# The MLPs' tiles of high and low weight parts begin 0 to 112 bytes further on

## The chip, the cores and the metric

The kernel runs on one core of a Trainium2 chip. The metric is the device time of one execution in microseconds (us), the median of several runs. The engines that matter here are TensorE (PE in the profile; its weight loads are PEld), VectorE (DVE), ScalarE (ACT) and the DMA queue of SyncE (SPq).

## What is computed

A two-layer transformer on 256 tokens of width 2,048 in float32: a layer with stick-breaking attention, a layer with native sparse attention, and behind each an MLP with a squared ReLU:

```python
def sqrelu_mlp(h, w1, w2):
    return jnp.square(jax.nn.relu(h @ w1)) @ w2        # w1: 2048 x 8192, w2: 8192 x 2048

for layer in range(2):
    h = h + attention[layer](rms_norm(h, ...))
    h = h + sqrelu_mlp(rms_norm(h, mlp_norm_g[layer]), mlp_w1[layer], mlp_w2[layer])
```

All weights are float32, some 400 MB, and each is read from memory once.

## The kernel before

**Split products.** TensorE multiplies numbers of type fp32r. To keep float32 accuracy each operand is split into a high part (the number rounded to fp32r) and a low part (what the rounding left). A product is then three: high by high, low by high, high by low. Activations are split once and stay in the tiles `xs` (high and low parts of the normed input side by side, 16 blocks of 128 rows, each 2 x 256 columns) and `yhi`, `ylo` (the MLP's hidden part). Weights come in chunks of 512 KB: `load` (L132) fetches one into one of five `raw` buffers, 128 partitions x 1,024 numbers, and `split` (L123 to L128) makes its parts: ScalarE copies `raw` into `hi` (L125), VectorE subtracts `hi` from `raw` into `lo` (L127). There are four buffers of each, taken in turn.

**The MLP.** Each MLP runs four rounds of `group1` and `group2`. `group1` makes 2,048 hidden columns in four blocks of 512, each from 8 chunks of `w1` in `proj_T2`: there the weights are the stationary operand, 8 matmuls of `hi` against 512 columns of `xs` (L193) and then 8 of `lo` against its 256 high columns (L199). `group2` multiplies with `w2`: 24 chunks go through `chunk_N`, where the activations are stationary and the weights move, 12 matmuls of 512 columns each (L147: `hi` against `yhi` and `ylo` in turn, then `lo` against `yhi`). Between these stand 8 chunks of one column block done with a Strassen scheme in `chunk_S`: 21 matmuls of 256 columns (L268). Three of its seven products use parts of the raw chunk, in the tiles `shi` and `slo`, which it splits by itself; the four others use sums of its quarters, `ts`, which go through `split` and so lie in `hi` and `lo` tiles. The stationary operand there is `ss` (sums of the activations) or `yhi`, `ylo`. Of the 12 matmuls with `hi` and `lo` tiles, 9 meet `ss` and 3 meet `yhi` or `ylo`. The list `order` in `group2` says in which order plain and Strassen chunks follow one another.

**Other users of `split`.** The attention layers' projections call it too: `chunk_T` (L176), `chunk_N` (L147) and `proj_T2h` (L213, L219).

**Where the tiles lie.** A tile is a stretch of bytes in each partition. In the built program, before and after, with the address modulo 128:

```
tile                      before                               after
xs                        32,896 (0)                           the same
yhi, ylo                  65,664 and 82,048 (0)                the same
raw, 5 buffers            108,480 + 4,096 b (64)               the same
hi, 4 buffers             128,960 + 4,096 b (64)               128,960 + 4,224 b (64) + offset
lo, 4 buffers             145,344 + 4,096 b (64)               145,856 + 4,224 b (64) + offset
ss                        161,728 (64)                         162,752 (64)
shi, slo                  218,048 and 221,120 (64)             219,072 and 222,144 (64)
```

Within a chunk all slices that a matmul takes begin a multiple of 512 bytes further on, so the address modulo 128 is that of the tile. In the attention layers some operands meet at other distances modulo 128: 0 on L642, L643 and L645; 0, 32, 64 and 96 in turn on L780 (`ws` moving, `bs` stationary); 32 on L919 and L920 where `vc` is an operand.

Of the kernel before, what the change touches and what calls it, by code (L numbers as in the profile page):

```python
# [9 lines left out]
F32R = mybir.dt.float32r  # L10
# [5 lines left out]
P = 128  # L16
# [3 lines left out]
KD = D // P  # L20
NB = 512
# [4 lines left out]
KC = 2  # L26
# [13 lines left out]
def hybrid_kernel(  # L40
# [10 lines left out]
    whi = ctx.enter_context(tc.tile_pool(name="whi", bufs=4))  # L51
    wlo = ctx.enter_context(tc.tile_pool(name="wlo", bufs=4))
# [52 lines left out]
    def pump():  # L105
        if beside:
            b = beside[0]
            b[2] += b[1] / KC
            while b[2] >= 1:
                b[2] -= 1  # L110
                y = next(b[0], b)
                if y is b:
                    beside.remove(b)
                if y:
                    break
# [4 lines left out]
                pass  # L120


    def split(raw):  # L123
        hi = whi.tile(raw.shape, F32R, tag="hi", name="hi")
        nc.scalar.activation(hi, raw, AF.Copy)  # L125
        lo = wlo.tile(raw.shape, F32R, tag="lo", name="lo")
        nc.vector.tensor_tensor(lo, raw, hi.bitcast(F32), op=OP.subtract)  # L127
        return hi, lo  # L128

# [7 lines left out]
    def load_split(*where):  # L137
        return split(load(*where))

    def bank(pool, tag):  # L140
        return pool.tile([P, NB], F32, tag=tag, name=tag)
# [44 lines left out]
    def proj_T2(ps, src, n0):  # L186


        for k0 in range(0, KD, KC):
            hi, lo = load_split(src, k0, KC, n0, NB)  # L190
            tiles = [(kk, m) for kk in range(KC) for m in range(NB // P)]
            for kk, m in tiles:
                nc.tensor.matmul(  # L193
                    ps[m], hi[:, kk, m * P:(m + 1) * P], xs[:, k0 + kk, :, :].rearrange("p a t -> p (a t)"),
                    start=k0 + kk == 0, stop=k0 + kk == KD - 1, skip_group_check=True,
                )
            pump()
            for kk, m in tiles:
                nc.tensor.matmul(  # L199
                    ps[m][:, :T], lo[:, kk, m * P:(m + 1) * P], xhi[:, k0 + kk, :],  # L200
                    start=False, stop=k0 + kk == KD - 1, skip_group_check=True,
                )
            pump()
# [75 lines left out]
    def banks_S(pool, tag):  # L279

        W = NB // 2
        bs = [bank(pool, tag) for _ in range(4)]
        half = lambda j, i: bs[j][:, i * W:(i + 1) * W]
        return bs, [half(0, 0), half(1, 0), half(1, 1), half(2, 0), half(2, 1), half(3, 1), half(3, 0)]
# [29 lines left out]
    def split_evac(hi, lo, src, scale=None):  # L314

        if scale is None:
            nc.scalar.activation(hi, src, AF.Copy)  # L317
            nc.vector.tensor_tensor(lo, src, hi.bitcast(F32), op=OP.subtract)  # L318
        else:
            nc.scalar.activation(hi, src, AF.Copy, scale=scale)  # L320
            nc.vector.scalar_tensor_tensor(
                lo, src, scale, hi.bitcast(F32), op0=OP.mult, op1=OP.subtract
            )
# [44 lines left out]
    def make_rstd(layer):  # L368
        s = small.tile([P, NT], F32, tag="ms", name="ms")
        nc.vector.tensor_reduce(s, ssq_t[layer], axis=AX.X, op=OP.add)  # L370
        nc.vector.tensor_scalar(s, s, 1.0 / D, EPS, op0=OP.mult, op1=OP.add)
        r = small.tile([P, NT], F32, tag="rstd", name="rstd")
        nc.gpsimd.tensor_tensor(r, s, neghalf[:, :NT], op=OP.pow)
        return r

    def bcast_rows(rstd):

        ps = bank(att, "att")
        for t in range(NT):
            nc.tensor.transpose(ps[:, t * P:(t + 1) * P], rstd[:, t:t + 1].to_broadcast([P, P]), ident)  # L380
        return ps
# [36 lines left out]
    def mlp(l, layer, junk, done, last=None):  # L418
        w1, w2 = mlp_w1[l], mlp_w2[l]
        ss = junk.tile([P, 2, KD // 2, 4, P], F32R, name="ss", bufs=1)  # L420
        row = junk.tile([P, T], F32, name="row", bufs=1)

        def rows():
            yield
            pb = bcast_rows(make_rstd(layer))
            nc.scalar.activation(row, pb[:, :T], AF.Copy)

        def group1(fg, pools):

            for fb in range(D // NB):  # L430
                ps = [bank(*pools[fb % 2]) for _ in range(NB // P)]
                proj_T2(ps, w1, fg * D + fb * NB)
                k, n = fb * (NB // P), NB // P
                a = junk.tile([P, n, T], F32, tag="pre", name="pre", bufs=1)
                for j in range(n):
                    c = junk.tile([P, T], F32, tag="part", name="part")
                    nc.scalar.activation(c, ps[j][:, T:], AF.Copy)
                    nc.vector.tensor_tensor(a[:, j, :], ps[j][:, :T], c, op=OP.add)
                nc.vector.scalar_tensor_tensor(
                    a, a, 0.0, row.unsqueeze(1).to_broadcast([P, n, T]), op0=OP.max, op1=OP.mult  # L440
                )
                s = junk.tile([P, n, T], F32, tag="sq", name="sq", bufs=1)
                nc.scalar.activation(s, a, AF.Square)
                nc.scalar.activation(yhi[:, k:k + n, :], s, AF.Copy)
                nc.vector.tensor_tensor(ylo[:, k:k + n, :], s, yhi[:, k:k + n, :].bitcast(F32), op=OP.subtract)

                sv = s.rearrange("p (j kk) t -> p j kk t", kk=2)
                a1, a2 = [[sv[:, :, kk, t * P:(t + 1) * P] for kk in (1, 0)] for t in range(NT)]
                q = junk.tile([P, 2, 4, P], F32, tag="sums", name="sums", bufs=1)
                nc.vector.scalar_tensor_tensor(q[:, :, 0, :], a2[0], -1.0, a2[1], op0=OP.mult, op1=OP.subtract)  # L450
                nc.vector.tensor_tensor(q[:, :, 2, :], a1[0], a2[0], op=OP.subtract)
                nc.vector.tensor_tensor(q[:, :, 1, :], a2[1], q[:, :, 2, :], op=OP.subtract)
                nc.vector.tensor_tensor(q[:, :, 3, :], a1[1], q[:, :, 1, :], op=OP.subtract)
                split_evac(ss[:, 0, k // 2:k // 2 + 2], ss[:, 1, k // 2:k // 2 + 2], q)

        def group2(fg, plain, strassen, end):

            NK = KD // KC
            order, si = [], 0
            for i in range(3 * NK):  # L460
                order.append(((0, 1, 3)[i // NK], i % NK))
                if si < NK and i >= (3 + 1.75 * si if end else 4 + 2.25 * si):
                    order.append((2, si))
                    si += 1
            for nb, i in order:
                k0 = fg * KD + i * KC
                args = (w2, k0, nb * NB, i == 0, i == NK - 1, yhi, ylo)
                if nb == 2:
                    if i == 0:
                        bs, s = banks_S(*strassen)  # L470
                    chunk_S(s, *args, ss[:, 0], ss[:, 1], koff=fg * KD)
                    if i == NK - 1:
                        add_S(nb, bs, s, junk)
                        if end:
                            for n in range(3):
                                done(n, strassen)
                    continue
                if i == 0:
                    ps = [bank(*plain) for _ in range(NT)]
                out = last is not None and end and nb == 3  # L480
                chunk_N(ps, w2, k0, nb * NB, i == 0, i == NK - (2 if out else 1), yhi, ylo, koff=fg * KD,
                        by_token=out and i == NK - 1)
                if i == NK - 1:
                    if out:
                        add_out(nb, ps, last)
                        return
                    add_h(nb, ps)
                    if end and nb == 3:
                        done(nb, plain)

        spawn(rows(), 1)
        A, B = (acc, "acc"), (att, "att")
        for fg in range(DFF // D):
            end = fg == DFF // D - 1
            group1(fg, ((A, B), (B, A))[fg % 2])
            group2(fg, *((A, B), (B, A))[fg % 2], end)
# [211 lines left out]
    with tc.tile_pool(name="nsa", bufs=2) as ap, ExitStack() as last:  # L708
# [270 lines left out]
        for k0 in range(0, KD, GK):  # L979
            raw = load(w_in, k0, GK, D + 6 * NB + GATES - P, P)  # L980
# [6 lines left out]
            for kk in range(GK):  # L987
                k = k0 + kk
# [40 lines left out]
        for g in range(G):  # L1029
            ps = [bank(acc, "acc") for _ in range(NT)]  # L1030
            for k0 in range(0, KD, KC):
                raw = wraw.tile([P, KC, NB], F32, tag="raw", name="raw")
# [61 lines left out]
```

## Time and profile before

| | us |
|---|---|
| median of 3 runs | 2201.02 (2199.73 to 2203.11) |
| the profiled execution | 2201.79 |
| its span, first to last instruction | 2200.1 |

The profile is of one execution. Its page gives each engine's busy time, the chain of work that ended last (followed back from the last instruction), and groups of instructions by line. Matmuls are pipelined: the record of one lasts past the start of the next, so the distance between two starts is shorter than a record.

### The profile page before, as it was taken

To read this page: it belongs to the slowest core of one execution; us is meant where nothing else is said; L and a number is where in the kernel's file an instruction comes from. 1 tells how busy PE (TensorE), PEld (TensorE's weight loads), DVE (VectorE), ACT (ScalarE), POOL (GpSimd) and SP (SyncE) were. 2 spreads that over 40 slices of the span, in tenths; PEclk is the share of its full clock that TensorE was granted. 3 is DMA by queue.
4 is the path that set the end of the run, shared out by engine and by line. 5 is a ranking of instruction groups with operands and counts; after the bars stand their busy time and mean duration, and the time that the engine had idled before them with its cause. 6 is when DMAs were issued, how large, how long until landed. Compare 5 with 4: busy or idle time off the path is not lost.

```text
span 2200.1 us, 31289 instructions
## 1 busy us (share of the span) xinstructions
PE 2187.0 (99%) x11922; PEld 1875.4 (85%) x11922; DVE 1537.9 (70%) x2096; ACT 1204.4 (55%) x1697; POOL 42.6 (2%) x75
## 2 busy tenths in 40 slices
PE   9999999999999999999999999999999999999998
PEld 9888888888888888888887888888888888888887
DVE  5656655677667677668777777756776776777775
ACT  5565665555455455455555666655554554554553
POOL 0000000000000000000000011000000000000000
PEclk9999999999999999999999999999999999999999
DMA  7655555665665665665667554456556656656654
GB/s 233 207 165 172 165 171 182 182 192 184 205 190 175 215 190 178 215 191 174 213 184 219 153 144 139 134 169 183 181 183 214 188 184 207 189 174 220 189 174 155
DMA packets 260767, 405.98 MB, mean 185 GB/s; under 512 B 13188, under 2 KB 91912, under 8 KB 260616
## 3 DMA queue, kind: packets, MB, share of 16 engines
q1 hardware_dynamic: 259800, 403.52, 60.2%
q8 instruction: 93, 1.52, 0.3%
q10 hardware_dynamic: 816, 0.46, 0.1%
q14 instruction: 58, 0.48, 0.1%
HBM read 401.83 MB, written 2.10 MB: 184 GB/s over the span
## 4 chain that ended last, share of the span: by engine, by line
PE 98%; DVE 1%; DMA 0%; POOL 0%; ACT 0%; issue 0%; DVEq 0%; ACTq 0%; POOLq 0%
PE acc L147 31%; PE att L147 13%; PE acc L193 11%; PE att L193 11%; PE acc L213 5%; PE acc L199 5%; PE att L199 5%; PE att L268 4%; PE acc L268 3%; PE acc L219 3%; PE acc L176 2%; PE att L926 1%; PE att L331 1%; PE att L918 0%; DMA raw<-in_mlp_w_dram 0%; PE att L919 0%
## 5 line engine op out<-in xcount | busy, mean ns | idle before, releaser
L127 DVE TENSOR_TENSOR lo<-raw,hi 128x1024 fp32r<-128x1024 f32 x687 | 836.6, 1222 | 380.3 <-ACT hi L125 358.1
L125 ACT ACTIVATE hi<-raw 128x1024 fp32r<-128x1024 f32 x687 | 724.8, 1057 | 656.3 <-PE acc L147 208.5
L193 PE MATMUL acc<-xs,hi 128*128 128x512 f32 x1024 | 259.8, 396 | 0.0
L193 PE MATMUL att<-xs,hi 128*128 128x512 f32 x1024 | 259.1, 395 | 0.0
L147 PE MATMUL acc<-hi,yhi 128*128 128x512 f32 x640 | 251.7, 394 | 0.0
L147 PE MATMUL acc<-hi,ylo 128*128 128x512 f32 x640 | 250.6, 392 | 0.0
L193 PEld LDWEIGHTS acc<-xs,hi 128*128 128x128 f32 x1024 | 183.0, 188 | 34.7 <-DVE h L387 0.3
L193 PEld LDWEIGHTS att<-xs,hi 128*128 128x128 f32 x1024 | 183.2, 188 | 34.5
L147 PE MATMUL acc<-hi,xs 128*128 128x512 f32 x704 | 178.6, 394 | 0.0
L147 PE MATMUL acc<-lo,yhi 128*128 128x512 f32 x640 | 174.1, 393 | 0.0
L147 PEld LDWEIGHTS acc<-hi,xs 128*128 128x128 f32 x704 | 130.5, 188 | 27.6
L147 PE MATMUL att<-hi,ylo 128*128 128x512 f32 x380 | 149.7, 394 | 0.0
L147 PE MATMUL att<-hi,yhi 128*128 128x512 f32 x380 | 149.4, 393 | 0.0
L199 PEld LDWEIGHTS acc<-xs,lo 128*128 128x128 f32 x1024 | 135.9, 188 | 11.6
L199 PEld LDWEIGHTS att<-xs,lo 128*128 128x128 f32 x1024 | 135.9, 188 | 11.6
L147 PEld LDWEIGHTS acc<-lo,yhi 128*128 128x128 f32 x640 | 119.6, 188 | 25.8 <-issue 0.4
L147 PEld LDWEIGHTS acc<-hi,ylo 128*128 128x128 f32 x640 | 120.3, 188 | 24.5 <-DVE ylo L318 0.2
L147 PEld LDWEIGHTS acc<-hi,yhi 128*128 128x128 f32 x640 | 120.2, 188 | 24.3 <-ACT yhi L317 0.2
L199 PE MATMUL acc<-xs,lo 128*128 128x256 f32 x1024 | 137.6, 277 | 0.0
L199 PE MATMUL att<-xs,lo 128*128 128x256 f32 x1024 | 137.5, 277 | 0.0
L243 DVE TENSOR_TENSOR ts<-raw 128x512 f32<-128x512 f32 x64 | 44.3, 692 | 128.9 <-DMA raw<-in_mlp_w_dram 128.9
L125 ACT ACTIVATE hi<-ts 128x1024 fp32r<-128x1024 f32 x64 | 67.9, 1061 | 114.4 <-DVE ts L248 86.3
(305 smaller groups left out, 3064.9 us busy)
## 6 DMA issues: line engine op xcount, KB each, us to landing
raw<-in_mlp_w_dram SPq DMA_DIRECT2D x512, 512.0 KB, 4.2
raw<-in_sb_w_qkv_dram SPq DMA_DIRECT2D x95, 512.0 KB, 4.2
raw<-in_nsa_w_in_dram SPq DMA_DIRECT2D x50, 512.0 KB, 3.6
raw<-in_sb_w_out_dram SPq DMA_DIRECT2D x32, 512.0 KB, 3.9
raw<-in_nsa_w_in_dram SPq DMA_DIRECT2D x64, 256.0 KB, 3.4
raw<-in_nsa_w_out_dram SPq DMA_DIRECT2D x32, 512.0 KB, 3.9
w1t<-in_nsa_cmp_w_dram SPq DMA_DIRECT2D x8, 512.0 KB, 4.8
h<-in_x_dram SPq DMA_DIRECT2D x8, 256.0 KB, 4.5
```

Source lines behind the costliest of these rows:

```text
L125: nc.scalar.activation(hi, raw, AF.Copy)
L127: nc.vector.tensor_tensor(lo, raw, hi.bitcast(F32), op=OP.subtract)
L147: mm = lambda a, b, k, t, s, e: nc.tensor.matmul(ps[t], a[:, k, t * P:(t + 1) * P], b, start=s, stop=e)
L176: nc.tensor.matmul(o, w[:, kk, m * P:(m + 1) * P], x[:, k0 + kk, :], start=s, stop=e, skip_group_check=True)
L193: nc.tensor.matmul(ps[m], hi[:, kk, m * P:(m + 1) * P], xs[:, k0 + kk, :, :].rearrange("p a t -> p (a t)"), start=k0 + kk == 0, stop=k0 + ...
L199: nc.tensor.matmul(ps[m][:, :T], lo[:, kk, m * P:(m + 1) * P], xhi[:, k0 + kk, :], start=False, stop=k0 + kk == KD - 1, skip_group_check=True,
L213: nc.tensor.matmul(ps[m], hi[:, kk, m * P:(m + 1) * P], xs[:, k0 + kk, :, :].rearrange("p a t -> p (a t)"), start=k0 + kk == 0, stop=k0 + ...
L219: nc.tensor.matmul(ps[m][:, :T], lo[:, kk, m * P:(m + 1) * P], xhi[:, k0 + kk, :], start=False, stop=k0 + kk == KD - 1, skip_group_check=True,
L243: nc.vector.tensor_tensor(ts[:, :2, :], flat[:, W:3 * W].rearrange("p (a n) -> p a n", a=2), b12, op=OP.subtract)
L268: nc.tensor.matmul(ps[i], a, w, start=s, stop=e, skip_group_check=True)
L331: nc.tensor.transpose(ps[:, j * T + t * P:j * T + (t + 1) * P], h[:, t, (kp + j) * P:(kp + j + 1) * P], ident)
L926: nc.tensor.transpose(ptp[:w, j * P:(j + 1) * P], src(j), ident)
```

## The change

`split` takes tiles of 1,024 + 32 numbers and uses 1,024 of them from an offset on. The offset comes from a list, `shift`, and is 0 where the list is empty. The MLP fills the list: in `group1` with 16 bytes x ((column block + chunk) modulo 8) for each chunk, in `group2` with 16 bytes x (place in the order modulo 8). High and low part of one chunk have the same offset. The order of the instructions on each engine is the same as before, and so are their waits. In the MLPs the address of `hi` and `lo` modulo 128 thus goes through all eight multiples of 16; on L193 and L199 each comes for one eighth of the matmuls.

```diff
+    shift = []
+
     def split(raw):
-        hi = whi.tile(raw.shape, F32R, tag="hi", name="hi")
+
+        n = KC * NB
+        o = shift.pop(0) if shift else 0
+        view = lambda t: t[:, o:o + n].rearrange("p (k n) -> p k n", k=raw.shape[1])
+        hi = view(whi.tile([P, n + 32], F32R, tag="hi", name="hi"))
         nc.scalar.activation(hi, raw, AF.Copy)
-        lo = wlo.tile(raw.shape, F32R, tag="lo", name="lo")
+        lo = view(wlo.tile([P, n + 32], F32R, tag="lo", name="lo"))
         nc.vector.tensor_tensor(lo, raw, hi.bitcast(F32), op=OP.subtract)
         return hi, lo
...
             for fb in range(D // NB):
                 ps = [bank(*pools[fb % 2]) for _ in range(NB // P)]
+                shift.extend(4 * ((fb + i) % 8) for i in range(KD // KC))
                 proj_T2(ps, w1, fg * D + fb * NB)
...
-            for nb, i in order:
+            for n, (nb, i) in enumerate(order):
+                shift.append(4 * (n % 8))
                 k0 = fg * KD + i * KC
```

## Rows read from the trace of the kernel before

**Rows 1.** the page: engines' busy time and share, and TensorE's granted clock by slice

```profile
PE 2187.0 (99%) x11922; PEld 1875.4 (85%) x11922; DVE 1537.9 (70%) x2096; ACT 1204.4 (55%) x1697; POOL 42.6 (2%) x75
...
PEclk9999999999999999999999999999999999999999
```

**Rows 2.** the page: the chain that ended last, its shares by engine

```profile
PE 98%; DVE 1%; DMA 0%; POOL 0%; ACT 0%; issue 0%; DVEq 0%; ACTq 0%; POOLq 0%
```

**Rows 3.** TensorE's waits, the longest of the list: us in total, times, longest

```profile
PE acc L268 <- DVE slo L249: 3.4, 3, 2.6
```

**Rows 4.** the chain from 600 to 640 us: start, length, what

```profile
602.79 0.91 PE acc L199 x8
603.70 1.86 PE acc L193 x8
```

**Rows 5.** the chain from 1060.9 to 1071 us

```profile
1061.12 5.49 PE att L147 x24
1066.61 2.46 PE acc L268 x21
```

**Rows 6.** the page's groups: busy us, mean ns of one | idle before

```profile
L127 DVE TENSOR_TENSOR lo<-raw,hi 128x1024 fp32r<-128x1024 f32 x687 | 836.6, 1222 | 380.3 <-ACT hi L125 358.1
L125 ACT ACTIVATE hi<-raw 128x1024 fp32r<-128x1024 f32 x687 | 724.8, 1057 | 656.3 <-PE acc L147 208.5
...
L193 PE MATMUL acc<-xs,hi 128*128 128x512 f32 x1024 | 259.8, 396 | 0.0
L193 PE MATMUL att<-xs,hi 128*128 128x512 f32 x1024 | 259.1, 395 | 0.0
...
L199 PE MATMUL acc<-xs,lo 128*128 128x256 f32 x1024 | 137.6, 277 | 0.0
```

**Rows 7.** L193 and L199: record's ns shortest/median/longest, first and last start

```profile
L193 PE MATMUL att<-xs,hi x1024: 388/396/398, 420.9 to 2081.7; 128*128 128x512 f32 x171
...
L199 PE MATMUL acc<-xs,lo x1024: 276/276/283, 399.4 to 2104.9; 128*128 128x256 f32 x171
```

**Rows 8.** L268: the same, two of its pairs

```profile
L268 PE MATMUL att<-hi,ss x192: 283/283/283, 501.9 to 2006.8; 128*128 128x256 f32 x192
...
L268 PE MATMUL att<-hi,yhi x32: 276/276/276, 502.6 to 2007.0; 128*128 128x256 f32 x32
```

**Rows 9.** L147 in the first MLP, 390 to 1102 us: busy, mean ns

```profile
L147 PE MATMUL acc<-hi,yhi 128*128 128x512 f32 x202 | 78.9, 391 | 0.0
...
L147 PE MATMUL att<-hi,ylo 128*128 128x512 f32 x192 | 75.2, 392 | 0.0
```

**Rows 10.** 256 columns at other distances: busy, mean ns

```profile
L780 PE MATMUL att<-ws,bs 128*120 128x256 f32 x64 | 9.1, 281 | 0.0
...
L645 PE MATMUL att<-sl,ones 128*128 128x256 f32 x8 | 2.2, 281 | 0.0
...
L645 PE MATMUL att<-sh,ones 128*128 128x256 f32 x8 | 2.2, 279 | 0.0
```

**Rows 11.** 512 columns at other distances: busy, mean ns

```profile
L642 PE MATMUL att<-sh,tri 128*128 128x512 f32 x8 | 3.2, 395 | 0.0
L643 PE MATMUL att<-sl,tri 128*128 128x512 f32 x8 | 3.1, 392 | 0.0
...
L920 PE MATMUL att<-pT,vc 8*128 8x512 f32 x4 | 1.6, 392 | 0.0
...
L919 PE MATMUL att<-pT,vc 8*128 8x512 f32 x4 | 1.5, 387 | 0.0
```

**Rows 12.** TensorE in order of time near 25 us: start, length, what

```profile
20.90 2.05 PE L176 MATMUL acc<-xs,hi 128*128 128x256 f32 x16
22.79 1.11 PE L176 MATMUL acc<-xs,lo 128*128 128x256 f32 x8
...
26.91 1.98 PE L176 MATMUL acc<-xs,hi 128*128 128x256 f32 x16
28.72 1.07 PE L176 MATMUL acc<-xs,lo 128*128 128x256 f32 x8
```

## The prediction, made before the changed kernel was run

> **What bounds the kernel now.** I read the page from the top. TensorE's row is at 99% of the span, in every slice at nine tenths or more and at the full clock (2.4 GHz) [rows 1]; the chain that ended last is 98% TensorE [rows 2]; and the list of TensorE's own waits is a few microseconds in all [rows 3]. So nothing that only moves work on VectorE, ScalarE or the DMA queues can change the time, unless it makes TensorE wait. What can change it is how far apart TensorE's matmuls start, and there are 11,922 of them [rows 1]: 1 ns on each would be 11.9 us.
>
> Next I read those distances from the chain of an MLP stage. A chunk of the first product is 8 matmuls of 512 columns in 1.86 us and 8 of 256 columns in 0.91 us [rows 4], so 232.5 and 113.8 ns apart. In the second product 24 matmuls of 512 columns take 5.49 us and the 21 of a Strassen chunk 2.46 us [rows 5], 228.8 and 117.1 ns apart. A record is longer than the distance to the next start by a fixed tail: L199's record is 277 ns [rows 6] against 113.8, L193's 395.5 (mean of 396 and 395) against 232.5, so 163 ns both times. Differences between records are therefore differences between distances, and from here I use records.
>
> The important rows are those of L268. One moving tile, `hi`, meets two stationary tiles there: with `ss` the records are 283 ns, shortest, median and longest alike, with `yhi` 276 ns [rows 8]. Width and type are the same. What differs is the address: `ss` and `hi` both begin 64 bytes past a multiple of 128, `yhi` begins at a multiple of 128. I call the distance of the stationary from the moving operand, modulo 128 bytes, the phase: it is 0 in the first pair, 64 in the second. That is the very quantity that this change turns.
>
> **The change part by part.** *What it does not touch.* No instruction is added, removed or moved on any engine: only addresses change. The five `raw` buffers stay where they were, so the DMAs are the same. The splits on ScalarE (1,057 ns) and VectorE (1,222 ns) [rows 6] write to shifted addresses; a chunk lasts 1.86 + 0.91 = 2.77 us, so VectorE has 1.5 us to spare per chunk before it could bind: I cost it at nothing. If a shifted write were to double the VectorE split to 2.4 us, a plain chunk would still hide it.
>
> *What it touches.* In the MLPs every one of the shifted tiles has had one constant phase against its partner: 64 with `xs`, `yhi`, `ylo`, and 0 with `ss`. Afterwards the phase goes through the eight multiples of 16, about equally often. The lowest records on L193 and L199 are 388 and 276 ns [rows 7]; I take these as the cost without any disturbance. Then the cost of today's phase above that floor is:
> - L193, 2,048 matmuls: 395.5 - 388 = 7.5 ns.
> - L199, 2,048 matmuls: 277 - 276 = 1 ns.
> - L147 in the MLPs (8 groups x 3 column blocks x 8 chunks x 12 = 2,304 matmuls): means of 391 and 392 [rows 9], taken as 392: 4 ns.
> - L268 with a shifted moving tile, 64 chunks x 9 with `ss` and x 3 with `yhi`, `ylo`: 7 ns for 576, 0 for 192.
>
> The trace does not show what the other phases cost in these streams. Bounds: from below each matmul at its floor, from above each at the highest usual record, 398 for 512 columns [rows 7] and 283 for 256 [rows 8]. Nearer rows are the places outside the MLPs that have other phases, in short sequences. With 256 columns: L780, whose phase steps by 32 bytes from matmul to matmul, 281; L645, at phase 0, 279 and 281 [rows 10]. I take 280.5, that is 4.5 ns above the floor, between the 276 and the 283 of [rows 8]. With 512 columns: L642 and L643 at phase 0, 395 and 392; L919 and L920 with `vc` at phase 32, 387 and 392 [rows 11]. I take 393.5, nearer to the full-array rows at phase 0, since the `vc` operands have 8 rows only.
>
> The sum:
> - L199: 2,048 x (280.5 - 277) = +7.2 us
> - L193: 2,048 x (393.5 - 395.5) = -4.1 us
> - L147: 2,304 x (393.5 - 392) = +3.5 us
> - L268 with `ss`: 576 x (280.5 - 283) = -1.4 us
> - L268 with `yhi`, `ylo`: 192 x (280.5 - 276) = +0.9 us
>
> Together +6.1 us. TensorE is on the chain all the time, so all of it counts. The profiled execution took 2201.8 us (span 2200.1 and 1.7 around it), 0.8 us above the median of 2201.0; against that median the forecast is 2207.1 us, 0.28% slower. The reason in a sentence: the 256-column matmuls of the first product have the luckiest phase now, and can only lose it, while the 512-column ones stand in the middle of their spread.
>
> *A side effect.* The buffers are now 4,224 instead of 4,096 bytes apart, so bit 7 of the address alternates from buffer to buffer for all chunks, the attention layers' too. Modulo 128 these keep their phase. If bit 7 counts, half of the 1,908 other matmuls on L147 would go from 392 towards L193's 395.5, 954 x 3.5 = +3.3 us, and half of L213's 512 the other way, -0.9: +2.4 us. I leave it out of the sum and in the range.
>
> **The rivals.** *The address does not matter: 2201 us.* The Trainium skill ("TensorE: Matmul & The Clock Gate", section "Step-by-step: what each phase is for") says that TensorE has two independent read ports, so that loading the next weights takes nothing from the running matmul; by that rule the time stays where it is, and the trace would have to have another cause for the 7 ns of L268. For it, from rows: L176, at the constant phase 64, has 16 matmuls from 20.90 to 22.79 us, 118 ns apart, and 16 others from 26.91 to 28.72, 113 ns apart [rows 12]: with the same phase two rhythms are possible, so the start of a stream counts too, and the phase may be only one of the causes. Against it: [rows 8], where the pairs alternate within each chunk, 64 times over.
>
> *The wide matmuls come out lower: not slower, about 2186 us.* If phase 64 is a poor one for 512 columns, most other phases would be at the floor: L193 loses 7.5 ns in seven of eight, 13.4 us, L147 4 ns, 8.1 us. If L199 and L268 lose as above (+6.7 us), the sum is -14.8: 2186 us. The point of decision: the change pays as soon as the 512-column matmuls average under 392.0 ns (4,352 of them; 6.7 us / 4,352 = 1.5 ns below their present mean, 393.6). Phase 32 on L919 and L920 with `vc` speaks for it, L642 against. Halfway to this case lies no change.
>
> *Every phase but 64 is bad: 2233 us.* L199 at 283, +12.3 us; L193 at 398, +5.1; L147 at 398, +13.8; L268's 192 at 283, +1.3; sum +32.5. It needs a conflict at nearly all distances; L645's 280 at phase 0 and L643's 392 speak against that.
>
> *The shift does not arrive.* The offsets are taken from a list, one for each split; if another consumer took one, the order would slip but the phases would still be mixed. It changes nothing in the sum.
>
> **How the numbers follow.** Forecast and its neighbours above the limit (2205.4 to 2224): 0.42; all phases bad: 0.05; within 0.2% of 2201.0, about what a measurement of this kernel can tell from no change (4.4 us either way), by the first rival or by gains and losses that cancel: 0.28; faster, by the second rival or part of it: 0.25. So faster 0.25, same 0.28, slower 0.47. The range leaves out half of the bad case, the top of the forecast's and the better half of the second rival's: 2188 to 2224. Slower alone is 2205 to 2224.
>
> **What would show it.** Records on L199 (its new line is 6 lines up) averaging about 280.5 instead of 277 confirm the largest term; L193's should come to 393 to 394, L147's to 393 or 394, L268's `ss` pairs to 280 or 281. If all means are as before, the first rival holds. If L193's or L147's fall to 390 or less while L199's stay under 280, the second. The chain should still be 98% TensorE; a VectorE or ScalarE split that appears there would make the part on the untouched engines wrong. TensorE's rows outside the MLPs must stay as they are, or bit 7 counts. The prediction is wrong if phases between 0 and 64 cost something quite unlike their two ends, which no row here shows.

## The result, and the profile after

The changed kernel takes 2216.49 us, median of three (2215.21 to 2217.9), against 2201.02 before: ratio 1.0069, 95% interval 1.0046 to 1.0092. It is 0.7% slower. The forecast was 2207 us and slower, the range 2188 to 2224. The profiled execution of after took 2215.21 us.

The page of after first: the busy times, and the chain that ended last with its shares by engine and by line. `split` and everything below it moved by 6 lines, so L147, L193, L199 and L268 are now L153, L199, L205 and L274.

```profile
PE 2203.3 (100%) x11922; PEld 1884.0 (85%) x11922; DVE 1538.4 (70%) x2096; ACT 1207.8 (55%) x1697; POOL 42.6 (2%) x75
...
PEclk9999999999999999999999999999999999999999
...
PE 97%; DVE 1%; DMA 1%; issue 0%; ACT 0%; POOL 0%; DVEq 0%; ACTq 0%; SPq 0%; POOLq 0%
PE acc L153 31%; PE att L153 12%; PE acc L199 11%; PE att L199 11%; PE att L205 5%; PE acc L205 5%; PE acc L219 5%; PE att L274 4%; PE acc L274 3%; PE acc L225 3%; PE acc L182 2%; DMA raw<-in_mlp_w_dram 1%; PE att L934 1%; PE att L337 1%; PE att L926 0%
...
L133 DVE TENSOR_TENSOR lo<-raw,hi 128x1024 fp32r<-128x1024 f32 x687 | 837.3, 1222 | 395.7 <-ACT hi L131 383.8
L131 ACT ACTIVATE hi<-raw 128x1024 fp32r<-128x1024 f32 x687 | 725.2, 1058 | 679.6 <-PE acc L153 227.3
```

TensorE is still the bound. Its busy time rose by 16.3 us (2187.0 in [rows 1]), the span by 13.4, and the number of its instructions and the granted clock are the same. The two splits, which write to the shifted addresses, take what they took: 1,222 and 1,058 ns against 1,222 and 1,057 in [rows 6]. So the extra time lies between TensorE's own matmuls.

The chain from 607 us on shows it in the first product (start, length, what); [rows 4] is its counterpart:

```profile
607.18 1.83 PE acc L199 x8
609.01 0.95 PE acc L205 x8
609.96 1.82 PE acc L199 x8
611.78 0.95 PE acc L205 x8
612.73 1.86 PE acc L199 x8
614.59 0.93 PE acc L205 x8
```

Before, each chunk was 1.86 and 0.91 us; now the 512-column half wavers between 1.82 and 1.86 from chunk to chunk, and the 256-column half takes 0.93 to 0.95. The groups by form say the same over the whole program (busy us and mean ns of one record, idle before):

```profile
L199 PE MATMUL acc<-xs,hi 128*128 128x512 f32 x1024 | 258.9, 395 | 0.0
L199 PE MATMUL att<-xs,hi 128*128 128x512 f32 x1024 | 258.2, 394 | 0.0
L153 PE MATMUL acc<-hi,yhi 128*128 128x512 f32 x640 | 253.4, 396 | 0.0
L153 PE MATMUL acc<-hi,ylo 128*128 128x512 f32 x640 | 252.1, 394 | 0.0
...
L153 PE MATMUL att<-hi,yhi 128*128 128x512 f32 x380 | 150.0, 395 | 0.0
L205 PE MATMUL att<-xs,lo 128*128 128x256 f32 x1024 | 141.6, 280 | 0.0
...
L225 PE MATMUL acc<-xs,lo 128*128 128x256 f32 x512 | 70.4, 280 | 0.0
```

The same groups of L153 before, when it was L147 ([rows 9] has the first MLP alone; these are the whole program):

```profile
L147 PE MATMUL acc<-hi,yhi 128*128 128x512 f32 x640 | 251.7, 394 | 0.0
L147 PE MATMUL acc<-hi,ylo 128*128 128x512 f32 x640 | 250.6, 392 | 0.0
...
L147 PE MATMUL att<-hi,yhi 128*128 128x512 f32 x380 | 149.4, 393 | 0.0
```

L205 went from 277 to 280 ns, L199 from 396 and 395 to 395 and 394 [rows 6], L153 from 394, 392 and 393 to 396, 394 and 395. L225 is not in an MLP: its tiles are not shifted by the list, and yet it is in this table, at 280 ns (278 before). The Strassen chunk, pair by pair (shortest/median/longest record), first after and then one pair before:

```profile
L274 PE MATMUL att<-hi,ss x192: 275/280/285, 504.1 to 2022.7; 128*128 128x256 f32 x192
...
L274 PE MATMUL att<-shi,yhi x64: 275/279/283, 503.4 to 2021.6; 128*128 128x256 f32 x64
...
L274 PE MATMUL att<-hi,yhi x32: 276/280/287, 504.8 to 2022.8; 128*128 128x256 f32 x32
```

```profile
L268 PE MATMUL att<-shi,yhi x64: 276/276/276, 501.2 to 2005.8; 128*128 128x256 f32 x64
```

The two clean values of [rows 8], 283 and 276 without spread, have both become 280 with a spread of ten. `shi` against `yhi` spreads too (275 to 283 ns, before 276 throughout), although neither tile changed its address modulo 256.

TensorE's waits hold one small gain (us in total, times, longest): before, `slo` cost 3.4 us [rows 3].

```profile
PE acc L274 <- DVE slo L255: 0.3, 1, 0.3
```

**The sum as measured.** I took from the traces, for each matmul that reads a weight tile, the time from its start to the next start, and call it the spacing. The few spacings of 300 ns and more are left out. Means before and after, times the number of matmuls:

| term | spacing, ns | measured, us | predicted, us |
|---|---|---|---|
| 256 columns against `xs` (L199, now L205), 2,048 | 114.0 to 117.9 | +8.1 | +7.2 |
| 512 columns against `xs` (L193, now L199), 2,048 | 232.8 to 231.9 | -1.8 | -4.1 |
| 512 moving columns in the MLPs (L147, now L153), 2,304 | 228.9 to 232.4 | +8.0 | +3.5 |
| Strassen, `hi` and `lo` with `ss`, 576 | 120.1 to 117.7 | -1.4 | -1.4 |
| Strassen, `hi` and `lo` with `yhi`, `ylo`, 192 | 113.4 to 118.9 | +1.0 | +0.9 |
| Strassen, `shi` and `slo`, all 576 | with `shi` and `yhi` 113.5 to 117.4 | +1.3 | not in the sum |
| attention layers (L147, L213, L219, L176 before) | | +2.5 | +2.4, left out of the sum |
| TensorE's wait for `slo` | | -3.1 | none |

That is +14.6 us; the span grew by 13.4, so 1.2 us are not accounted for.

### The profile page after: what moved, and what is told of

It reads as the page before. It is cut to its first block, busy times and chain, and to the rows that moved or that the text cites. A ratio compares the mean times of both kernels' runs of the same rounds, so it can differ in the third digit from the quotient of the medians.

```text
span 2213.5 us, 31289 instructions
## 1 busy us (share of the span) xinstructions
PE 2203.3 (100%) x11922; PEld 1884.0 (85%) x11922; DVE 1538.4 (70%) x2096; ACT 1207.8 (55%) x1697; POOL 42.6 (2%) x75
## 4 chain that ended last, share of the span: by engine, by line
PE 97%; DVE 1%; DMA 1%; issue 0%; ACT 0%; POOL 0%; DVEq 0%; ACTq 0%; SPq 0%; POOLq 0%
PE acc L153 31%; PE att L153 12%; PE acc L199 11%; PE att L199 11%; PE att L205 5%; PE acc L205 5%; PE acc L219 5%; PE att L274 4%; PE acc L274 3%; PE acc L225 3%; PE acc L182 2%; DMA raw<-in_mlp_w_dram 1%; PE att L934 1%; PE att L337 1%; PE att L926 0%
## 5 line engine op out<-in xcount | busy, mean ns | idle before, releaser
L133 DVE TENSOR_TENSOR lo<-raw,hi 128x1024 fp32r<-128x1024 f32 x687 | 837.3, 1222 | 395.7 <-ACT hi L131 383.8
L131 ACT ACTIVATE hi<-raw 128x1024 fp32r<-128x1024 f32 x687 | 725.2, 1058 | 679.6 <-PE acc L153 227.3
L199 PE MATMUL acc<-xs,hi 128*128 128x512 f32 x1024 | 258.9, 395 | 0.0
L199 PE MATMUL att<-xs,hi 128*128 128x512 f32 x1024 | 258.2, 394 | 0.0
L153 PE MATMUL acc<-hi,yhi 128*128 128x512 f32 x640 | 253.4, 396 | 0.0
L153 PE MATMUL acc<-hi,ylo 128*128 128x512 f32 x640 | 252.1, 394 | 0.0
L199 PEld LDWEIGHTS att<-xs,hi 128*128 128x128 f32 x1024 | 183.7, 188 | 34.2
L199 PEld LDWEIGHTS acc<-xs,hi 128*128 128x128 f32 x1024 | 183.5, 188 | 34.4 <-DVE h L393 0.3
L153 PE MATMUL acc<-hi,xs 128*128 128x512 f32 x704 | 179.3, 395 | 0.0
L153 PE MATMUL acc<-lo,yhi 128*128 128x512 f32 x640 | 175.4, 395 | 0.0
L153 PEld LDWEIGHTS acc<-hi,xs 128*128 128x128 f32 x704 | 130.4, 188 | 28.4
L153 PE MATMUL att<-hi,ylo 128*128 128x512 f32 x380 | 150.0, 395 | 0.0
L153 PE MATMUL att<-hi,yhi 128*128 128x512 f32 x380 | 150.0, 395 | 0.0
L205 PEld LDWEIGHTS att<-xs,lo 128*128 128x128 f32 x1024 | 138.8, 188 | 11.2
L205 PEld LDWEIGHTS acc<-xs,lo 128*128 128x128 f32 x1024 | 138.7, 188 | 11.2
L153 PEld LDWEIGHTS acc<-lo,yhi 128*128 128x128 f32 x640 | 119.7, 188 | 27.6 <-issue 0.4
L153 PEld LDWEIGHTS acc<-hi,ylo 128*128 128x128 f32 x640 | 120.4, 188 | 25.7 <-DVE ylo L324 0.2
L153 PEld LDWEIGHTS acc<-hi,yhi 128*128 128x128 f32 x640 | 120.3, 188 | 25.8 <-ACT yhi L323 0.2
L205 PE MATMUL att<-xs,lo 128*128 128x256 f32 x1024 | 141.6, 280 | 0.0
L205 PE MATMUL acc<-xs,lo 128*128 128x256 f32 x1024 | 141.5, 280 | 0.0
L219 PE MATMUL acc<-xs,hi 128*128 128x512 f32 x512 | 129.8, 396 | 0.0
```

What stands on the lines that cost most here:

```text
L153: mm = lambda a, b, k, t, s, e: nc.tensor.matmul(ps[t], a[:, k, t * P:(t + 1) * P], b, start=s, stop=e)
L199: nc.tensor.matmul(ps[m], hi[:, kk, m * P:(m + 1) * P], xs[:, k0 + kk, :, :].rearrange("p a t -> p (a t)"), start=k0 + kk == 0, stop=k0 + ...
L205: nc.tensor.matmul(ps[m][:, :T], lo[:, kk, m * P:(m + 1) * P], xhi[:, k0 + kk, :], start=False, stop=k0 + kk == KD - 1, skip_group_check=True,
L219: nc.tensor.matmul(ps[m], hi[:, kk, m * P:(m + 1) * P], xs[:, k0 + kk, :, :].rearrange("p a t -> p (a t)"), start=k0 + kk == 0, stop=k0 + ...
```

## The phase has a period of 256 bytes

From here on **phase** is the address of the stationary operand minus that of the moving one, modulo 256 instead of 128, and **spacing** is the time from one start to the next.

Sorted by phase, the trace of after shows that distances that are equal modulo 128 cost different times, and distances equal modulo 256 the same. For the 512-column matmuls against `xs`, with the distance taken modulo 512:

```
distance mod 512       0       256     64      320     144     400     192     448     240     496
spacing, ns (mean)     228.64  228.66  232.8   232.9   229.75  229.73  230.3   230.6   228.9   229.0
```

0 and 128 differ (228.65 and 233.0 ns), 64 and 192 differ (232.9 and 230.5), but 0 and 256, 64 and 320 agree to a tenth or two. The prediction had counted modulo 128, and its side effect is then no side effect: buffers 4,224 bytes apart turn the phase by 128 from one to the next, in the MLPs and in the attention layers.

Four theories went into the experiments.
- **A**: the distance modulo 128 sets the price, as the prediction had it.
- **B**: the distance modulo 256 sets it, and each matmul pays for its own.
- **R**: no distance is dear by itself; turning it from chunk to chunk costs.
- **Rhythm**: a phase allows more than one spacing, and the stream ahead decides which one is taken. [rows 12] had shown 118 and 113 ns at one phase.

In each experiment all engines run the same instructions in the same order as before. What differs is where tiles lie.

## Experiments on the cause

**Pitch alone.** Tiles 128 bytes longer, no offsets.

```diff
-        hi = whi.tile(raw.shape, F32R, tag="hi", name="hi")
+        n = KC * NB
+        view = lambda t, o: t[:, o:o + n].rearrange("p (k n) -> p k n", k=raw.shape[1])
+        hi = view(whi.tile([P, n + 32], F32R, tag="hi", name="hi"), 0)
```

(the same for `lo`.)

> Only the distance between buffers is the change's, 4,224 bytes instead of 4,096; every offset is 0. The address modulo 128 is what it was, bit 7 alternates from buffer to buffer. Theory A (the phase counts modulo 128, as the prediction had it): nothing moves, 2201 us, L149 keeps a mean record of 392 ns and L201 one of 277. Theory B (the phase counts modulo 256, as the means of the changed kernel by phase suggest): half of the chunks with moving weights go from distance 192 to 64, where the changed kernel's starts are 233 instead of 229.5 ns apart, +8 us; half of the 256-column matmuls of the first product go to 192, 117 instead of 114 ns, +6 us; its 512-column ones gain 3 us. Sum 8 to 13 us: 2209 to 2214 us.

Measured: 2211.74 us against 2199.53, ratio 1.0053 (1.0040 to 1.0066). The groups by form:

```profile
L149 PE MATMUL acc<-hi,yhi 128*128 128x512 f32 x640 | 253.4, 396 | 0.0
...
L201 PE MATMUL att<-xs,lo 128*128 128x256 f32 x1024 | 140.4, 279 | 0.0
```

A is out: nothing changed modulo 128, and three quarters of the loss are there. Split by phase, the half of the buffers that stayed at the old phase and the half that moved by 128 differ where the columns are 512: at 64 the spacing is 232.6 ns (`xs` moving), 233.9 (`hi` moving against `yhi`) and 231.5 (against `ylo`), at 192 it is 230.4, 229.6 and 229.8. 64 is the dearer phase whichever operand moves. With `lo` moving against `yhi` the two are only 0.6 ns apart (231.3 and 230.7).

**A constant gap of 96 bytes.** An unused tile ahead of the weight tiles; no phase changes from chunk to chunk.

```diff
+    gap = ctx.enter_context(tc.tile_pool(name="gap", bufs=1))
     whi = ctx.enter_context(tc.tile_pool(name="whi", bufs=4))
...
+    gap_t = gap.tile([P, 24], F32, name="gap_t")
```

> No offset and no new distance between buffers: an unused gap of 96 bytes ahead of the hi pool moves hi, lo and all that lies behind by a constant. The distance to xs goes from 64 to 160, that of the moving weights from 192 to 96 (modulo 256), for the attention layers too; ss moves along and keeps distance 0. Theory B (a phase has its price by itself): the price at 160 and 96 in the changed kernel, 119.8 ns for 256 columns (+12 to +15 us with L222) and 234 ns for moving weights (+17 to +20 us): 2230 to 2237 us. Theory R (what costs is that the phase changes from chunk to chunk, and any constant phase settles at the low rhythm): 2199 to 2204 us.

Measured: 2237.18 us against 2199.53, ratio 1.0170 (1.0156 to 1.0184).

```profile
L195 PE MATMUL acc<-xs,hi 128*128 128x512 f32 x1024 | 260.2, 395 | 0.0
...
L149 PE MATMUL acc<-hi,yhi 128*128 128x512 f32 x640 | 254.7, 398 | 0.0
...
L201 PE MATMUL att<-xs,lo 128*128 128x256 f32 x1024 | 143.7, 282 | 0.0
```

R is out: with constant phases (160 against `xs`, 96 for moving weights) the kernel is slower than the change that turns them. 256 columns: 120.4 ns instead of 114.2, times 2,688 with the attention layers, 16.6 us. The 4,212 wide matmuls with moving weights: 3 to 5.4 ns more each, 19.1 us. With 512 columns against `xs` 0.4 ns, 1.0 us. Together 36.7 of the 37.7 us.

**Constant gaps of 128 and 256 bytes.** The same tile with 32 and with 64 numbers. The first exchanges the phases 64 and 192; the second changes nothing modulo 256.

> A gap of 128 bytes ahead of the hi pool and nothing else: distances modulo 128 are those of before, modulo 256 they turn round, xs with hi and lo at 192 instead of 64, moving weights at 64 instead of 192, in all layers, constant. Theory A (modulo 128): 2200 us. Theory B (modulo 256): moving weights 233 instead of 229.5 ns, 4,212 x 3.5 = +15 us; 512 columns against xs 230.4 instead of 232.8, 2,560 x 2.4 = -6 us; 256 columns against xs at 117.5 instead of 114, +9 us, or unchanged if they find the low rhythm: 2208 to 2218 us.

> A gap of 256 bytes ahead of the hi pool and nothing else: all distances modulo 256 are those of before, modulo 512 they turn round. Theory B (the period is 256 bytes): 2198 to 2202 us, the same records. If a longer period counts: a time as unlike 2200 as the run with 128 bytes.

Measured: with 128 bytes 2212.21 us against 2199.97, ratio 1.0054 (1.0041 to 1.0066); with 256 bytes 2199.43, ratio 0.9996 (0.9986 to 1.0005). The chain in the first product, first with 128 bytes, then with 256:

```profile
604.96 0.91 PE acc L201 x8
605.87 1.83 PE acc L195 x8
607.70 0.94 PE acc L201 x8
```

```profile
601.53 0.91 PE acc L201 x8
602.45 1.86 PE acc L195 x8
604.31 0.91 PE acc L201 x8
```

With 256 bytes the chunk is that of [rows 4] to the hundredth. With 128 bytes the 512-column half falls from 1.86 to 1.83 us (232.8 to 229.2 ns apart), while the weights that move rise from 228.7 to 230.6 ns to 233.0 to 233.4, and the 256-column half alternates between 0.91 and 0.94. In us: -9.1, +15.5 and +5.1, together +11.5; measured +12.2. This pair is the cleanest evidence for the period of 256, and for the price of 64 (233 ns) against 192 (229 to 231) at 512 columns.

The gap of 128 bytes also tells the distance from the address. `hi` and `ss` both move by 128 bytes there, so their distance stays 0, and their record stays 283 ns; `hi` against `yhi`, where `hi` alone moved, goes from 276 to 281:

```profile
L270 PE MATMUL att<-hi,ss x192: 281/283/283, 505.7 to 2019.7; 128*128 128x256 f32 x192
...
L270 PE MATMUL att<-hi,yhi x32: 281/281/281, 506.4 to 2019.8; 128*128 128x256 f32 x32
```

**Offsets alone.** The change's offsets, in buffers 4,352 = 17 x 256 bytes apart, so that the attention layers keep their phases. The room comes from sharing buffers (`u` and `v` of `add_S` in one tile "pre", one buffer of `pc` less).

```diff
+        hi = view(whi.tile([P, n + 64], F32R, tag="hi", name="hi"), o)
...
+                shift.extend(4 * ((fb + i) % 8) for i in range(KD // KC))
...
+                shift.append(4 * (n % 8))
```

> The offsets of the change, 0 to 112 bytes in turn, but buffers 4,352 bytes apart, so that bit 7 is the same in all buffers; the attention layers keep their distances modulo 256. (The room is made by letting add_S use a pre tile and by one buffer less of pc.) Theory B: the turn alone, by the means at the distances 64 to 176 and 192 to 80: 256 columns +9 us, moving weights +6 us, 512 columns of the first product -1 us: 2212 to 2217 us, about as slow as the change, though by other phases. Theory A: the prediction's +6 us, 2207 us, the rest being the distance between buffers. If the distance between buffers does it all: 2201 us.

Measured: 2214.56 us against 2199.53, ratio 1.0067 (1.0054 to 1.0079).

```profile
L204 PE MATMUL att<-xs,lo 128*128 128x256 f32 x1024 | 141.6, 281 | 0.0
```

The offsets alone cost as much as the whole change, and the pitch alone three quarters of it. The two don't add: either mixes the phases, and the two mixtures cost much the same (12.2 and 15.0 us).

**`ss` alone, by 64 bytes.** The counter-test: an edit that should gain. `ss` is put 64 bytes further on, so that its phase against `hi` and `lo` is 64 instead of 0.

```diff
-        ss = junk.tile([P, 2, KD // 2, 4, P], F32R, name="ss", bufs=1)
+        ss = junk.tile([P, KD * 4 * P + 64], F32R, name="ss", bufs=1)
+        ss = ss[:, 16:16 + KD * 4 * P].rearrange("p (a k i q) -> p a k i q", a=2, k=KD // 2, i=4)
```

> Of the kernel before only ss moves, by 64 bytes (in a tile 256 bytes longer, so that what lies behind keeps its place modulo 256). All other distances are those of before, and the Strassen chunks are entered as before, at distance 192. Theory B (the distance of the pair sets the price): the twelve matmuls with ss in each of 64 chunks go from 120.0 to 113.4 ns, -5 us: 2194 to 2196 us, records on L268 with ss 276 to 277 instead of 283. If the two rhythms at one distance decide (both 113.3 and 117.7 ns were seen at 64), some of them come out at 117.7: 2197 to 2199 us. If something other than the address of ss made its 7 ns, nothing moves.

Measured: 2196.23 us against 2199.97, ratio 0.9981 (0.9973 to 0.9990).

```profile
L268 PE MATMUL att<-hi,ss x192: 276/276/282, 503.5 to 2007.0; 128*128 128x256 f32 x192
...
L268 PE MATMUL att<-lo,ss x96: 276/276/285, 504.8 to 2007.9; 128*128 128x256 f32 x96
```

283 became 276: the two values of [rows 8] are one, and 3.7 us are gained where 576 + 192 matmuls x 6 ns (`shi` and `slo` meet `ss` too) make 4.6. So the address is the cause of the 7 ns, and the first rival is out. The Trainium skill ("TensorE: Matmul & The Clock Gate", section "Step-by-step: what each phase is for") says that loading the next weights takes no read bandwidth from the running matmul. By that sentence alone the distance between the two operands would not matter; here nothing but the address of `ss` changed, and its matmuls came 6 ns closer together. Which reads meet, the run does not tell.

## Experiments on what the price depends on besides

If each phase had its own price, the best kernel could be put together from the table of after. Four attempts.

**`hi` of the first product at phase 0** (228.65 ns in the trace of after), with `lo` left at 64. The offset is 192 bytes in `group1` alone, with the room again from `u` and `v`; `ss` moves by 64 and all behind it by 128 bytes, so that `shi` and `slo` meet `yhi` and `ylo` at 64.

```diff
+                shift.extend(48 for i in range(KD // KC))
                 proj_T2(ps, w1, fg * D + fb * NB)
```

> Two constant phases chosen by what was read: hi of the first product 192 bytes further on (distance 0 to xs, 228.7 instead of 232.8 ns in the changed kernel), lo where it was (distance 64, 114 ns); ss 64 bytes and all behind it 128 bytes further on, so that no Strassen pair stands at distance 0. Theory B: first product 2,048 x 4.1 = -8.4 us; Strassen pairs with ss, 768 x (120.0 - 113.4) = -5.1 us: 2188 us. If the start of a stream counts as much as the phase, L204 loses what it had (113.4 to 117.5, +8 us) and the sum is -5 us or less: 2196 us or more. If the address of ss does not matter, its records stay 283 ns.

Measured: 2200.27 us against 2199.53, ratio 1.0002 (0.9993 to 1.0012). The chain:

```profile
600.75 1.84 PE acc L198 x8
602.58 0.94 PE acc L204 x8
603.53 1.84 PE acc L198 x8
```

`hi` did what was wanted: 229.7 ns instead of 232.8, -6.3 us. But the matmuls with `lo` in the first product, whose phase is 64 as before, went from 114.0 to 117.7 ns, +7.7 us, and the gain was gone. (The 117.1 of later expectations is a mean with the attention layers, where `hi` had not moved.) Chunk by chunk, the eight with `lo` average under 114.2 ns in 249 of 256 chunks before, and 117 to 118 in 248 of 256 here. In the Strassen chunk `shi` against `yhi`, at phase 64 here, has 117.5 ns, `hi` against `ss` at 64 has 114.4 and `lo` against `ss` at 64 again 117.4. One phase, two rhythms: the rhythm theory has what a price by phase alone has not.

**`ylo` alone, by 64 bytes**, so that `ylo` meets the weights at 0 and `yhi` stays at 192.

```diff
-    ylo = cpool.tile([P, KD, T], F32R, name="ylo")
+    ylo = cpool.tile([P, KD * T + 64], F32R, name="ylo")
+    ylo = ylo[:, 16:16 + KD * T].rearrange("p (k t) -> p k t", k=KD)
```

> Of the kernel before only ylo moves, by 64 bytes: hi meets yhi at distance 192 as before and ylo at 0. Theory B with prices by distance alone: 0 cost 229.8 ns with moving weights in the changed kernel against 229.5 at 192, so nothing for the 1,020 pairs on L148, and 113.4 to 119 for the 256 with ylo on L269, +1.4 us: 2200 to 2203 us. If the alternation of two distances breaks the rhythm of three starts (226, 229, 232 ns) that the plain chunks now have, the 3,060 matmuls move by up to 3 ns either way: 2191 or 2209 us.

Measured: 2203.89 us against 2199.97, ratio 1.0016 (1.0007 to 1.0025).

```profile
L269 PE MATMUL att<-hi,yhi x32: 277/278/278, 503.3 to 2012.0; 128*128 128x256 f32 x32
L269 PE MATMUL att<-hi,ylo x32: 284/284/284, 503.4 to 2012.1; 128*128 128x256 f32 x32
```

In the plain chunks, where `yhi` and `ylo` alternate, `ylo`'s matmuls fell by 0.4 ns (229.2 to 228.8) and those of `yhi`, which had not been touched, rose by 2.7 (228.7 to 231.4). In the Strassen chunk `ylo` at phase 0 has 284 ns, one more than `ss` at 0 [rows 8]. A matmul's spacing is set by its neighbour's address too.

**`hi` at 144, and `hi` at 240**, both with `ss` at 64 and `lo` at 64. The edit is that of the attempt at 0, with 20 and 44 in place of 48, and with a tile for `ss` that is 256 bytes longer instead of 128, so that `shi` and `slo` keep their phases.

> The kernel with ss moved by 64 bytes, and hi of the first product 80 bytes further on (distance 144 to xs, 229.7 ns in the changed kernel and 227.9 in the run with the turn alone, against 232.8 at 64); lo stays at 64. Price by distance alone: 2,048 x 3 to 4.9 = -6 to -10 us against the kernel with ss moved: 2186 to 2190 us. If the 256-column matmuls take their rhythm from the stream ahead of them, as in the run with hi at distance 0 (117.1 instead of 114 at an unchanged 64), they give back 2,048 x 3 = 6 us: 2192 to 2198 us.

> The same with hi of the first product at distance 240 to xs (176 bytes further on), 228.9 ns in the changed kernel against 232.8 at 64; lo stays at 64. Price by distance alone: 2,048 x 3.9 = -8 us against the kernel with ss moved: 2188 us. If L204 falls into its other rhythm, 117 instead of 114 ns, 6 us come back: 2194 us; with both at the means of the run with hi at distance 0: 2196 us.

Measured: at 144 2200.70 us against 2200.12, ratio 1.0005 (0.9996 to 1.0014); at 240 2192.86, ratio 0.9968 (0.9955 to 0.9980). First the groups at 144, then the chain at 240:

```profile
L198 PE MATMUL acc<-xs,hi 128*128 128x512 f32 x1024 | 260.5, 396 | 0.0
...
L204 PE MATMUL att<-xs,lo 128*128 128x256 f32 x1024 | 140.1, 279 | 0.0
```

```profile
599.92 1.83 PE acc L198 x8
601.75 0.91 PE acc L204 x8
602.66 1.84 PE acc L198 x8
604.50 0.94 PE acc L204 x8
```

144 is a miss: 229.7 ns in the mixture of after, 233.4 ns here, where it is constant and `lo` stands at 64. 240 gave 229.5 ns for `hi` (228.9 in after), and `lo`'s half alternates between 0.91 and 0.94 us from chunk to chunk: the two rhythms side by side, in one stream at one phase. (From chunk to chunk the distance modulo 512 alternates here as well; with the gap of 128 bytes it does not, and the half alternates just the same.)

**Do the two gains add?** `hi` at 240 alone, and the kernel with both edits a second time beside it.

> Only hi of the first product stands 176 bytes further on (distance 240 from xs); ss stays at distance 0 from the moving tiles. If the gains of the two edits add, this run keeps what hi gave in the run with both: the 512-column records of the first product at 392 to 393 instead of 395.5 (about 3 ns x 2,048 = 6 us), the 256-column ones behind them at 279 instead of 277 (-1.6 ns x 2,048 = -3 us back), so 2196 to 2199 against 2200 before, and the pairs with ss at 283. If the whole gain of both came from hi, 2191 to 2195. If all of it came from ss, 2199 to 2202.

> The same kernel as the run with both edits (ss 64 bytes further, hi of the first product at 240), a second time beside the run with hi alone: 2190 to 2196 if the first result (ratio 0.9968) holds, and 3 to 5 us below the run with hi alone if the gains add; within 1.5 us of it if they do not.

Measured against 2199.94 us: `hi` alone 2197.97, ratio 0.9990 (0.9981 to 0.9999); both 2195.09, ratio 0.9975 (0.9965 to 0.9986). With `hi` alone:

```profile
L198 PE MATMUL acc<-xs,hi 128*128 128x512 f32 x1024 | 256.5, 393 | 0.0
...
L204 PE MATMUL att<-xs,lo 128*128 128x256 f32 x1024 | 139.6, 279 | 0.0
```

```profile
L273 PE MATMUL att<-hi,ss x192: 280/283/287, 501.7 to 2006.0; 128*128 128x256 f32 x192
```

They add, within what these medians can tell: 2.0 us for `hi`, 2.9 more for `ss` (3.7 by itself). From the spacings `hi` gains 3.2 ns x 2,048 = 6.6 us and `lo` gives 1.9 ns x 2,048 = 3.9 us back. The version with both is faster than both kernels, in both runs, by 0.25 and 0.32%.

Constant phases only, what the runs gave (spacing in ns; "before" is the kernel before):

| phase | 512 columns | 256 columns |
|---|---|---|
| 0 | 229.7 (`hi` in the first product); 228.8 (`ylo`) | 120.1 (`ss`, before) |
| 64 | 232.8 (before); 233.0 to 233.4 (gap of 128) | 114.0 (`lo`, before); 113.8 (`ss` at 64); 115.9 (`lo`, `hi` ahead at 240); 116.5 (at 144); 117.7 (at 0) |
| 96 | 233.7 to 234.4 (gap of 96) | 116.7 (`yhi`, gap of 96) |
| 144 | 233.4 | |
| 160 | 233.2 (gap of 96) | 120.4 (gap of 96) |
| 192 | 228.7 to 230.6 (before); 229.2 (gap of 128) | 113.4 (`yhi`, before); 116.1 (gap of 128) |
| 240 | 229.5 | |

## Why the prediction was right, and where its steps were not

The direction was right, and 2216.49 us lies in the range. The size was not: +0.28% was forecast and +0.69% measured, and the range held it because it had been drawn to 2224. The reason given, that L199 can only lose, accounts for 8.1 us; of the 8.0 us that L147 lost, 4.5 come from a step that failed.

- **What bounds the kernel: right.** The chain is 97% TensorE, the splits are unchanged, and among TensorE's waits is no transfer. The 1% of transfers on the chain comes from 2121 to 2161 us, where the chain is followed back through TensorE's one wait for `slo`, 0.3 us long. That this wait fell by 3.1 us is chance in good part: the kernel with `hi` at 240 and `ss` at 64 had 0.8 us of it in one profile and 3.6 in the other.
- **The rows of L268 as the key: right.** The 7 ns between `ss` and `yhi` is an address effect; moving `ss` alone took it away.
- **"Modulo 128 these keep their phase": wrong.** The period is 256. This is the step that failed. It put L193 and L199 (64) and L147 (192) at one phase, where there are two with different prices, and made the new pitch look like a side effect; by itself the pitch costs 0.53%. For the attention layers, left out of the sum, it had +2.4 us and +2.5 were measured, but that is luck: L147 there lost 2.4 us (forecast 3.3), L213 gained 0.5 (forecast 0.9), and L219, which was not in it, lost 1.1.
- **256 columns: right.** 280.5 ns was taken for a mixed phase, 280 measured; L199 had indeed a cheap place and lost 8.1 us (7.2). `ss` and `yhi` came out to a tenth.
- **512 columns: mis-sized.** 393.5 ns was taken for a mixed phase, from rows of the attention layers in short sequences. The MLPs show 394 to 395: against `xs` the phases 0, 144, 192 and 240 are cheap (228.7 to 230.6 ns), and the others cost 231 to 233.4. Nor was 388 ns a cost without disturbance: before, it is the record of the first of the eight in a chunk (242 of 256 chunks), and at the same phase the next seven alternate between 398 and 393. L193 therefore gained 1.8 us instead of 4.1, and L147, which stood at 192, lost 8.0 instead of 3.5. From the +6.1 us of the sum to the +13.4 of the span it is these 6.8 us, 1.0 of the 256-column terms, 2.5 of the attention layers and 1.3 of `shi` and `slo`, less 3.1 for the wait that shrank and 1.2 not accounted for.
- **Not foreseen: neighbours.** `shi` and `slo` kept their addresses modulo 256 and became slower by 1.3 us, as `yhi` did when only `ylo` was moved.
- **The rivals.** That the address does not matter is out. That the wide matmuls come out low was true of L193 at four of sixteen phases and the contrary of the truth for L147. That nearly every phase is bad is not so for a mixture; a constant gap of 96 bytes was as slow as that (2237 us against 2233), but with the attention layers in it, which the 2233 had not.

**What stays open.** The runs show that spacing depends on the distance of two addresses modulo 256, and on the neighbouring matmuls. Which two reads meet, if it is reads, is not shown. That the load of the next weights disturbs the running matmul would be the nearest guess, but the starts in the trace of before do not bear it out; there the price goes with a matmul's own two operands. The last matmul in a row of `hi` with `ss` has its own distance at 0 and the next weights at 192, and still takes 120.9 ns; the last of `shi` with `ylo` has 192 and the next weights at 0, and takes 113.6. Why a stream at one phase takes 113.4 ns in one chunk and about 117.7 in the next was not settled, nor why 144 was cheap in the mixture and dear by itself; in the trace of after 144 took 227.5 ns in the first MLP and 232.0 in the second, so the phase alone does not set it there either.

## What to carry to other kernels

Where TensorE is the bound and its chain has no waits, look for one matmul shape with two record lengths, and compare the addresses of stationary and moving tile modulo 256: `ss`, 64 bytes further on, gave 0.2% for two lines. Any edit that changes a tile's size can shift all tiles behind it, and a gap of 96 unused bytes cost 1.7%; so compare two versions at equal addresses modulo 256, or a difference under 2% may be the layout. Choose a constant phase by measurement in its place, not from a table, and don't rotate: here both mixtures cost more (12.2 and 15.0 us) than the constant phases of before.

## What the runs showed of the hardware that was not expected

- At 512 columns, the distance 64, where it is constant, gives 233 ns between starts and 192 gives 229 to 231, whichever operand moves; 256 bytes more change nothing (2199.43 against 2199.97 us).
- At 256 columns there are two rhythms, about 113.4 and 117.7 ns, at one and the same distance; which of them holds can change from chunk to chunk (0.91 and 0.94 us for eight).
- A matmul's spacing depends on its neighbour's address: 228.7 to 231.4 ns for `yhi` when `ylo` alone was moved.
